# First product of the convolution and the square of the GELU moved to ScalarE in the recurrent tiles of a decoder step

## The chip, the cores and the metric

The kernel runs on 1 core of one Trainium2 chip. The metric is the device time of one execution in microseconds (us); lower is better. All arithmetic is fp32; matrix products are made of three products of split operands (high by high, high by low, low by high).

## The reference

One inference step of one decoder layer, for a prompt of 1024 tokens and 64 sample tokens (8 sequences of 8) with the same weights: half-step FFN, RMS norm, one input projection `z = h @ w_in`, then three branches (dilated window attention, a recurrent branch, attention into a memory), a gated merge, an output projection, a second half-step FFN and a final norm. The change lies in the recurrent branch, of width 768:

```python
xc, conv_new = causal_conv(xr, conv_buf, conv_w, conv_b)       # width 4, per channel: sum_k w[k]*x[t+k-3] + b
r = sigmoid(xc @ w_a + b_a); i = sigmoid(xc @ w_i + b_i)       # 12 blocks of 64
log_a = -8 * r * softplus(-lam); a = exp(log_a)
u = sqrt(-expm1(2*log_a)) * (i * xc)
h_t = a_t * h_{t-1} + u_t                                      # scan over the positions
y_rec = gelu(yr) * h                                           # 0.5*y*(1+tanh(c*(y + 0.044715*y^3)))
```

## The kernel before

Tokens lie on the free axis (1088 columns, `NT`), features on the 128 partitions. The 1088 columns are worked in three chunks, `CH`, of 352, 368 and 368 columns. `z_tile` (L652) makes one block of 128 output features of the input projection: for each chunk, 24 matmuls (`mac3`, 8 blocks of k by three products) into one PSUM bank, then the evacuation function of the caller, then a `tick`. A tick (L71) also falls inside each `mac3`, so there are two ticks per chunk. At a tick the jobs that `later(n, f)` has put n ticks ahead are written out, and so are the next steps of side jobs: the merging of the attention groups (`att_combine`, L826), and the attention of the sample rows into their caches (`sample_job`, L917), which takes place on all engines in the same stage.

The order of instructions on PE, ScalarE (ACT), VectorE (DVE) and GpSimd (POOL) is the order in which the program writes them (`manual_schedule`, L1568): an engine that waits for an operand holds up all that stands behind it in its own queue.

The weights are loaded raw (`wr`), and `part` (L162) splits each into a high part on ScalarE (L167) and a low part on VectorE (L168); a ring of 7 split tiles (`ws`) stands ahead of PE.

The recurrent stage has 6 tiles of 128 features (`lru_tile`, L1297), each followed by one or two gate tiles (`gate_evac`, L1389), which are ordinary `z_tile`s. One recurrent tile is two `z_tile`s. The first has `conv` as its evacuation: L1312 scales the PSUM bank into `xe`, L1318 makes the first product of the convolution with its bias, and L1321 adds the other three products. Five ticks after, `gates(c)` issues two matmuls on the convolved chunk (L1332, three PSUM banks named `g`) and two sigmoids (L1333). The second `z_tile` has `gelu`: L1367 scales the bank into `Y`, and three POOL instructions (L1369 to L1371) make `y + 0.044715*y^3` in `G`.

After `gates(2)`, at the end of the GELU's second chunk, six jobs follow one tick apart: `tanh` (in the middle of the GELU's last chunk), then `power` (written just behind that chunk's evacuation: L1343, L1345), `root` (L1348), `grow` (L1351), `forcing` and `scan` (L1360). The tanh of the GELU (L1373) and the last products (L1374, L1378) come six to eight ticks after the last chunk, and the tile's result goes to DRAM.

PSUM in this stage: three banks for `z`, two named `t` for transposes and the sample rows, three `g`.

Of the kernel before, what the change touches and what calls it, by code (L numbers as in the profile page):

```python
# [11 lines left out]
AF = mybir.ActivationFunctionType  # L12
OP = mybir.AluOpType
# [21 lines left out]
GELU_C = math.sqrt(2.0 / math.pi)  # L35
# [25 lines left out]
class Kernel:  # L61
# [1235 lines left out]
    def lru_tile(self, i):  # L1297

        nc, p, w = self.nc, self.lp, self.lws[i % 2]
        T = lambda tag, n=LP: p.tile([128, n], F32, name=self.uid(tag), tag=tag, bufs=1)  # L1300
        xe, xc, A, B, S, Y, G = (T(x, n) for x, n in (("xe", LP + 3), ("xc", LP), ("lA", LP), ("lB", LP + 3), ("lS", LP),
                                                      ("lY", NT), ("lG", NT)))
        fin = p.tile([128, 36], F32, name=self.uid("fin"), tag="fin", bufs=1)
        smp = lambda ap: ap[:, SEQ + 3:SEQ + 91].rearrange("p (b u) -> p b u", u=11)
        samp = lambda ap: ap.rearrange("p (b t) -> p b t", b=8)
        nc.gpsimd.memset(xe[:, 0:3], 0.0)
        nc.gpsimd.tensor_copy(smp(xe)[:, :, 0:3], samp(self.stT[:, i, 0:24]))

        def conv(c, ps):
            t0, n = CH[c]  # L1310
            m = min(n, SEQ - t0)
            nc.vector.tensor_tensor(out=xe[:, 3 + t0:3 + t0 + m], in0=ps[:, :m], in1=self.rbc[:, t0:t0 + m], op=OP.mult)  # L1312
            if m < n:
                nc.vector.tensor_tensor(out=smp(xe)[:, :, 3:], in0=samp(ps[:, m:n]), in1=samp(self.rbc[:, SEQ:]),
                                        op=OP.mult)
            a, W = LCH[c]
            xo = xc[:, a:a + W]
            nc.vector.tensor_scalar(xo, xe[:, a:a + W], self.col("conv_w", i), self.col("conv_b", i),  # L1318
                                    op0=OP.mult, op1=OP.add)
            for k in range(1, 4):  # L1320
                nc.vector.scalar_tensor_tensor(xo, xe[:, a + k:a + k + W], self.col("conv_w", k * KR + i), xo,  # L1321
                                               op0=OP.mult, op1=OP.add)
            if m < n:
                nc.gpsimd.tensor_copy(fin[:, 0:3], xe[:, SEQ:SEQ + 3])
                nc.gpsimd.tensor_copy(fin[:, 3:27].rearrange("p (b w) -> p b w", b=8), smp(xe)[:, :, 8:11])
            self.later(5, lambda: gates(c))

        def gates(c):
            a, W = LCH[c]
            for j, (dst, name) in enumerate(((A, "lru_b_a"), (B, "lru_b_i"))):  # L1330
                pg = self.bank("g")
                nc.tensor.matmul(pg[:, :W], w[:, j, :], xc[:, a:a + W], start=True, stop=True)  # L1332
                nc.scalar.activation(dst[:, a:a + W], pg[:, :W], AF.Sigmoid, bias=self.col(name, i))  # L1333
            if c == 2:
                for n, f in enumerate((tanh, power, root, grow, forcing, scan)):
                    self.later(1 + n, f)

        def tanh():
            nc.scalar.activation(S, A, AF.Tanh, scale=self.c4[:, i:i + 1])
            nc.vector.tensor_tensor(out=xc, in0=xc, in1=B[:, :LP], op=OP.mult)  # L1340

        def power():
            nc.scalar.activation(A, A, AF.Exp, scale=self.cq[:, i:i + 1])  # L1343
            for _ in range(2):
                nc.scalar.activation(A, A, AF.Square)  # L1345

        def root():
            nc.scalar.activation(S, S, AF.Sqrt)  # L1348

        def grow():  # L1350
            nc.vector.scalar_tensor_tensor(S, A, 1.0, S, op0=OP.add, op1=OP.mult)  # L1351

        def forcing():
            nc.vector.tensor_tensor(out=S, in0=S, in1=xc, op=OP.mult)
            starts = slice(SEQ + 2, SEQ + 80, 11)
            nc.vector.memset(A[:, starts], 0.0)
            nc.vector.tensor_copy(S[:, starts], self.stT[:, i, 24:32])

        def scan():
            nc.vector.tensor_tensor_scan(B[:, :LP], A, S, 0.0, op0=OP.mult, op1=OP.add)  # L1360
            nc.gpsimd.tensor_copy(fin[:, 27:28], B[:, SEQ - 1:SEQ])
            nc.gpsimd.tensor_copy(fin[:, 28:36], B[:, SEQ + 10:SEQ + 88:11])
            nc.sync.dma_start(self.o["fin"][i], fin)

        def gelu(c, ps):
            t0, n = CH[c]
            nc.vector.tensor_tensor(out=Y[:, t0:t0 + n], in0=ps[:, :n], in1=self.rbc[:, t0:t0 + n], op=OP.mult)  # L1367
            y, g = Y[:, t0:t0 + n], G[:, t0:t0 + n]
            nc.gpsimd.tensor_tensor(out=g, in0=y, in1=y, op=OP.mult)  # L1369
            nc.gpsimd.tensor_scalar(g, g, 0.044715, 1.0, op0=OP.mult, op1=OP.add)  # L1370
            nc.gpsimd.tensor_tensor(out=g, in0=g, in1=y, op=OP.mult)  # L1371
            if c == 2:
                self.later(6, lambda: nc.scalar.activation(G, G, AF.Tanh, scale=GELU_C))  # L1373
                self.later(7, lambda: nc.vector.scalar_tensor_tensor(Y, G, 1.0, Y, op0=OP.add, op1=OP.mult))  # L1374
                self.later(8, gated)

        def gated():
            nc.vector.scalar_tensor_tensor(Y[:, :SEQ], Y[:, :SEQ], 0.5, B[:, :SEQ], op0=OP.mult, op1=OP.mult)  # L1378
            nc.vector.scalar_tensor_tensor(samp(Y[:, SEQ:]), samp(Y[:, SEQ:]), 0.5, smp(B)[:, :, 0:8],
                                           op0=OP.mult, op1=OP.mult)  # L1380
            nc.sync.dma_start(self.y_d[6 + i], Y)

        self.z_tile(conv)
        if i + 1 < KR:
            self.lru_weights(i + 1)
        self.z_tile(gelu)


# [570 lines left out]
```

## Time and profile before

| what | us |
|---|---|
| median of the three runs | 2753.1 |
| lowest of the three runs | 2748.8 |
| the profiled execution, its own time | 2744.7 |
| span of the profiled execution (first to last instruction) | 2742.9 |
| mean granted TensorE clock of the profiled execution, of full speed | 0.99 |

The profiled execution is one more run, taken with the profiler; its own time is 1.8 us above its span. The rows below come from it. PE is the matmul engine and PEld its weight loads, which overlap; DVE is VectorE, ACT is ScalarE, POOL is GpSimd, SP the queue of most DMAs. "Idle before" is the time in which an engine stood still ahead of an instruction, with the instruction that ended it.

### The profile page before, as it was taken

The numbers are of one execution on the slowest core, as the hardware profiler recorded it, in microseconds if no ns is written. First come the engines' busy times: TensorE is split into PE (matmuls) and PEld (weight loads), VectorE is DVE, ScalarE is ACT, GpSimd is POOL, SyncE is SP. The second block draws the span as 40 slices with busy tenths as digits, with TensorE's granted clock in tenths as the row PEclk, the third lists the DMA queues.
The fourth block names the chain that finished last, engine by engine and source line by source line (L and its number), as shares of the span: only waits on it lengthen the run. The fifth ranks groups of instructions, "written<-read, shape, count | busy, mean of one in ns | idle before, by whom it ended". The sixth has DMA issues, their size and how long they took to land.

```text
span 2742.9 us, 46310 instructions
## 1 busy us (share of the span) xinstructions
PE 2657.4 (97%) x18088; PEld 2576.8 (94%) x18088; DVE 1718.3 (63%) x3032; ACT 923.3 (34%) x1779; POOL 818.2 (30%) x743
## 2 busy tenths in 40 slices
PE   8999999899999999999989999999999999999997
PEld 7999999899999899989978889999999999999997
DVE  7666566777774433556587755863666566576776
ACT  7232323311153312333334533522542232242112
POOL 1365545200030000324353411231025555552003
PEclk9999999999999999999999999999999999999998
DMA  4222323522243252655544443754424455445221
GB/s 150 70 94 84 103 101 108 205 95 93 75 163 129 89 156 75 204 184 161 177 154 135 138 135 97 264 176 161 149 99 174 163 186 189 168 158 173 95 73 66
DMA packets 181404, 374.98 MB, mean 137 GB/s; under 512 B 21768, under 2 KB 116168, under 8 KB 180416
## 3 DMA queue, kind: packets, MB, share of 16 engines
q1 hardware_dynamic: 166464, 303.85, 33.6%
q0 software_dynamic: 2048, 43.65, 4.7%
q10 hardware_dynamic: 12672, 24.52, 2.4%
q8 instruction: 142, 2.33, 0.4%
q14 instruction: 78, 0.64, 0.1%
HBM read 305.59 MB, written 113.16 MB: 153 GB/s over the span
## 4 chain that ended last, share of the span: by engine, by line
PE 82%; DVE 9%; ACT 3%; issue 2%; DMA 2%; POOL 1%; SPq 0%; DVEq 0%; ACTq 0%; POOLq 0%
PE pg L262 9%; PE pg L264 9%; PE pg L263 9%; PE z L262 7%; PE z L263 7%; PE z L264 7%; PE pd L262 6%; PE pd L263 6%; PE pd L264 6%; DVE ws L168 2%; PE po L264 2%; PE po L263 2%; PE po L262 2%; PE wo L262 1%; PE wo L263 1%
## 5 line engine op out<-in xcount | busy, mean ns | idle before, releaser
L262 PE MATMUL pg<-xo,ws 128*128 128x272 f32 x2512 | 729.4, 290 | 19.8 <-DVE uu L539 10.9
L264 PE MATMUL pg<-xo,ws 128*128 128x272 f32 x2512 | 726.1, 289 | 6.1 <-DVE ws L168 6.1
L263 PE MATMUL pg<-xo,ws 128*128 128x272 f32 x2512 | 725.8, 289 | 0.0
L167 ACT ACTIVATE ws<-wr 128x512 fp32r<-128x512 f32 (+1 forms) x550 | 325.4, 613 | 844.7 <-PE pd L264 363.7
L168 DVE TENSOR_TENSOR ws<-wr,ws 128x512 fp32r<-128x512 f32 (+1 forms) x550 | 436.6, 816 | 137.4 <-ACT ws L167 136.8
L262 PEld LDWEIGHTS pg<-xo,ws 128*128 128x128 f32 x2512 | 475.6, 189 | 23.0 <-DVE uu L539 13.0
L264 PEld LDWEIGHTS pg<-xo,ws 128*128 128x128 f32 x2512 | 475.7, 189 | 7.0 <-DVE ws L168 6.9
L262 PE MATMUL z<-xg,ws 128*128 128x368 f32 (+1 forms) x1392 | 477.4, 343 | 0.0
L263 PEld LDWEIGHTS pg<-xo,ws 128*128 128x128 f32 x2512 | 475.9, 189 | 0.0
L264 PE MATMUL z<-xg,ws 128*128 128x368 f32 (+1 forms) x1392 | 459.0, 330 | 0.0
L263 PE MATMUL z<-xg,ws 128*128 128x368 f32 (+1 forms) x1392 | 458.8, 330 | 0.0
L262 PE MATMUL pd<-h,ws 128*128 128x368 f32 (+1 forms) x1056 | 347.3, 329 | 5.6 <-DVE x L648 4.5
L263 PE MATMUL pd<-h,ws 128*128 128x368 f32 (+1 forms) x1056 | 346.1, 328 | 0.0
L264 PE MATMUL pd<-h,ws 128*128 128x368 f32 (+1 forms) x1056 | 345.0, 327 | 0.0
L648 DVE TENSOR_TENSOR x<-x,pd 128x368 f32<-128x368 f32 (+1 forms) x504 | 257.7, 529 | 137.7 <-PE pd L264 136.0
L262 PEld LDWEIGHTS z<-xg,ws 128*128 128x128 f32 x1392 | 264.1, 190 | 15.6 <-issue 13.9
L263 PEld LDWEIGHTS z<-xg,ws 128*128 128x128 f32 x1392 | 264.3, 190 | 1.3
L264 PEld LDWEIGHTS z<-xg,ws 128*128 128x128 f32 x1392 | 263.4, 189 | 0.0
L262 PEld LDWEIGHTS pd<-h,ws 128*128 128x128 f32 x1056 | 198.1, 188 | 6.5 <-DVE x L648 5.1
L264 PEld LDWEIGHTS pd<-h,ws 128*128 128x128 f32 x1056 | 198.7, 188 | 0.0
L263 PEld LDWEIGHTS pd<-h,ws 128*128 128x128 f32 x1056 | 198.4, 188 | 0.0
L978 POOL TENSOR_TENSOR qb<-qb,kv 128x1024 f32<-128x1024 f32 x48 | 116.3, 2424 | 194.2 <-DMA qb<-qs_d 152.3
(295 smaller groups left out, 3692.3 us busy)
## 6 DMA issues: line engine op xcount, KB each, us to landing
wr<-in_w_gu_dram SPq DMA_DIRECT2D x96, 512.0 KB
wr<-in_w_in_dram SPq DMA_DIRECT2D x58, 512.0 KB
qb<-qs_d SPq DMA_DIRECT2D x48, 512.0 KB
h_d<-sl ACTq DMA_DIRECT2D x88, 272.0 KB
hr<-h_d SPq DMA_DIRECT2D x44, 544.0 KB
wr<-in_w_dn_dram SPq DMA_DIRECT2D x44, 512.0 KB
out_sk_dram<-in_cache_k_dram POOLq DMA_DIRECT2D x16, 1020.0 KB, 7.0
out_sv_dram<-in_cache_v_dram POOLq DMA_DIRECT2D x16, 1020.0 KB, 8.2
```

The costliest lines, as they stand in the source:

```text
L167: nc.scalar.activation(spl[:, 0, :n], src, AF.Copy)
L168: nc.vector.tensor_tensor(out=spl[:, 1, :n], in0=src, in1=spl[:, 0, :n].bitcast(F32), op=OP.subtract)
L262: nc.tensor.matmul(out, wh, xh, start=start and i == 0, stop=False, **more)
L263: nc.tensor.matmul(out, wh, xl, start=False, stop=False, **more)
L264: nc.tensor.matmul(out, wl, xh, start=False, stop=i == n - 1, **more)
L648: nc.vector.tensor_tensor(out=xa, in0=xa, in1=ps[:, :n], op=OP.add)
L978: nc.gpsimd.tensor_tensor(out=prev, in0=prev, in1=kk, op=OP.mult)
```

## The change

In `conv`, the first product with its bias goes from a VectorE `tensor_scalar` to one ScalarE activation (Identity, with scale and bias read per partition). In `gelu`, the POOL instructions are dropped: the square is a ScalarE activation, and one VectorE instruction makes `(y^2 + 1/0.044715) * y`; the factor 0.044715 goes into the scale of the tanh that follows. Nothing else moves: each new instruction is written at the place of the old one.

```diff
-            nc.vector.tensor_scalar(xo, xe[:, a:a + W], self.col("conv_w", i), self.col("conv_b", i),
-                                    op0=OP.mult, op1=OP.add)
+            nc.scalar.activation(xo, xe[:, a:a + W], AF.Identity, bias=self.col("conv_b", i), scale=self.col("conv_w", i))
             for k in range(1, 4):
                 nc.vector.scalar_tensor_tensor(xo, xe[:, a + k:a + k + W], self.col("conv_w", k * KR + i), xo,
                                                op0=OP.mult, op1=OP.add)
...
             y, g = Y[:, t0:t0 + n], G[:, t0:t0 + n]
-            nc.gpsimd.tensor_tensor(out=g, in0=y, in1=y, op=OP.mult)
-            nc.gpsimd.tensor_scalar(g, g, 0.044715, 1.0, op0=OP.mult, op1=OP.add)
-            nc.gpsimd.tensor_tensor(out=g, in0=g, in1=y, op=OP.mult)
+            nc.scalar.activation(g, y, AF.Square)
+            nc.vector.scalar_tensor_tensor(g, g, 1 / 0.044715, y, op0=OP.add, op1=OP.mult)
             if c == 2:
-                self.later(6, lambda: nc.scalar.activation(G, G, AF.Tanh, scale=GELU_C))
+                self.later(6, lambda: nc.scalar.activation(G, G, AF.Tanh, scale=GELU_C * 0.044715))
```

## Rows read from the trace of the kernel before

**Rows 1.** The page's first part: busy time, share of the span and number of instructions of each engine over the whole run.

```profile
PE 2657.4 (97%) x18088; PEld 2576.8 (94%) x18088; DVE 1718.3 (63%) x3032; ACT 923.3 (34%) x1779; POOL 818.2 (30%) x743
```

**Rows 2.** Busy time of each engine in stretches of the recurrent stage (1380 to 1700 us; the view of windows). Columns: stretch and its length, busy us (instructions) of PE, PEld, DVE, ACT and POOL, granted TensorE clock, busy share of the DMA engines, GB/s.

```profile
1380.00:1700.00 320.00, 300.25 (x1858) 269.63 (x1857) 218.34 (x432) 142.72 (x207) 110.76 (x152) 0.98 0.40 124
...
1380.00:1430.00 50.00, 38.98 (x224) 36.62 (x222) 43.98 (x63) 20.35 (x25) 32.51 (x25) 0.96 0.45 143
1580.00:1630.00 50.00, 50.00 (x324) 43.74 (x323) 25.31 (x48) 21.61 (x31) 8.67 (x12) 1.00 0.44 138
1430.00:1435.00 5.00, 2.95 (x11) 2.91 (x12) 2.99 (x6) 3.53 (x8) 2.13 (x8) 0.50 0.08 23
1490.00:1495.00 5.00, 5.00 (x22) 5.00 (x22) 2.06 (x11) 2.01 (x5) 3.22 (x5) 0.66 0.44 112
```

**Rows 3.** What the matmul engine PE waited for between 1375 and 1700 us (the view of waits): who waited and for whom, total us, times, longest us.

```profile
PE t L1020 <- ACT ss L1012: 8.9, 1, 8.9
PE g L1332 <- DVE xc L1321: 4.2, 2, 2.7
PE t L835 <- DVE ss L1009: 3.5, 1, 3.5
PE t L835 <- DVE sel L1047: 2.9, 2, 2.0
```

**Rows 4.** The instructions that the change removes or feeds, each asked by its line: number, shortest/median/longest duration in ns, first and last start in us, shapes.

```profile
L1318 DVE TENSOR_SCALAR xc<-xe,vec x18: 462/471/2380, 1384.8 to 1661.3; 128x352 f32<-128x352 f32 x6, 128x368 f32<-128x368 f32 x6, 128x392 f32<-128x392 f32 x6
L1321 DVE SCALAR_TENSOR_TENSOR xc<-xe,vec,xc x54: 583/602/2627, 1387.3 to 1663.2; 128x352 f32<-128x352 f32 x18, 128x368 f32<-128x368 f32 x18, 128x392 f32<-128x392 f32 x18
L1369 POOL TENSOR_TENSOR lG<-lY x18: 773/800/912, 1403.9 to 1677.1; 128x368 f32<-128x368 f32 x12, 128x352 f32<-128x352 f32 x6
L1370 POOL TENSOR_SCALAR lG<-lG x18: 487/500/821, 1404.8 to 1678.0; 128x368 f32<-128x368 f32 x12, 128x352 f32<-128x352 f32 x6
L1371 POOL TENSOR_TENSOR lG<-lG,lY x18: 940/985/2007, 1405.4 to 1678.6; 128x368 f32<-128x368 f32 x12, 128x352 f32<-128x352 f32 x6
```

**Rows 5.** ScalarE operations of the nearest shapes (the view of groups by line, shapes kept apart): count, busy us, mean ns, then idle us before them and its releasers. L1453 has no per-partition pointer operand, L281 has one (its scale), L319 is a square, the last row is one table load.

```profile
L1453 ACT ACTIVATE xg<-ta 128x368 fp32r<-128x368 f32 x16 | 8.2, 513 | 24.7 <-POOL ta L1465 24.7
L281 ACT ACTIVATE xg<-x,vec 128x368 fp32r<-128x368 f32 x16 | 9.6, 600 | 5.5 <-DVE x L648 4.8 <-DVE rs L290 0.8
L319 ACT ACTIVATE td<-x 128x368 f32<-128x368 f32 x25 | 12.6, 504 | 7.4 <-POOL acc L321 4.0 <-DVE x L648 2.3 <-DVE rs L290 1.1
L1348 ACT ACT_TABLE_LOAD x6 | 7.7, 1283 | 0.1
```

**Rows 6.** Single instructions of POOL and VectorE (DVE) in the first recurrent tile (the view by time): start us, length us, engine and line, operation, tiles and shapes, count, and in brackets the idle time before it with its releaser.

```profile
1384.63 2.38 POOL L978 TENSOR_TENSOR qb<-qb,kv 128x1024 f32<-128x1024 f32 x1 [0.27 <-DMA qb<-qs_d]
1384.84 2.38 DVE L1318 TENSOR_SCALAR xc<-xe,vec 128x352 f32<-128x352 f32 x1
1414.57 1.22 DVE L968 TENSOR_REDUCE sst<-qb 128x16 f32<-128x1024 f32 x1 [2.80 <-POOL qb L978]
1418.64 2.60 DVE L1351 SCALAR_TENSOR_TENSOR lS<-lA,lS 128x1112 f32<-128x1112 f32 x1 [0.41 <-ACT lS L1348]
```

**Rows 7.** The same view in the second recurrent tile, ScalarE (ACT), VectorE and PE: the table load with which the chain of exponentials begins, the evacuation of the GELU's last chunk, a later evacuation, and the wait of PE at the tile's end.

```profile
1457.46 1.28 ACT L1343 ACT_TABLE_LOAD   x1
1460.55 0.54 DVE L1367 TENSOR_TENSOR lY<-z,rbc 128x368 f32<-128x368 f32 x1 [1.87 <-PE z L264]
1469.99 0.54 DVE L1393 TENSOR_TENSOR ta<-z,rbc 128x368 f32<-128x368 f32 x1 [1.08 <-PE z L264]
1489.00 0.21 DVE L1009 TENSOR_TENSOR ss<-t,sbn 128x64 f32<-128x64 f32 x1
1489.23 0.41 PE L835 MATMUL t<-ident,oc 128*128 128x128 f32 x2 [3.49 <-DVE ss L1009]
```

**Rows 8.** The same view in the other tiles (first, third, fourth, fifth, sixth): the first ScalarE instruction of the chain of exponentials (L1343) and the evacuation of the GELU's last chunk (L1367).

```profile
1410.27 1.28 ACT L1343 ACT_TABLE_LOAD   x1
1411.24 0.53 DVE L1367 TENSOR_TENSOR lY<-z,rbc 128x368 f32<-128x368 f32 x1
1513.13 1.23 ACT L1343 ACTIVATE lA<-lA,spw 128x1112 f32<-128x1112 f32 x1
1561.84 1.23 ACT L1343 ACTIVATE lA<-lA,spw 128x1112 f32<-128x1112 f32 x1
1562.27 0.54 DVE L1367 TENSOR_TENSOR lY<-z,rbc 128x368 f32<-128x368 f32 x1
1616.66 1.28 ACT L1343 ACT_TABLE_LOAD   x1
1619.27 0.54 DVE L1367 TENSOR_TENSOR lY<-z,rbc 128x368 f32<-128x368 f32 x1 [2.86 <-PE z L264]
1674.20 1.28 ACT L1343 ACT_TABLE_LOAD   x1
1676.51 0.54 DVE L1367 TENSOR_TENSOR lY<-z,rbc 128x368 f32<-128x368 f32 x1 [2.09 <-PE z L264]
```

**Rows 9.** The same view, in the fifth tile the instruction that frees a PSUM bank and the matmuls that take that bank next, and in the sixth tile the transposes at the end of the sample rows' attention.

```profile
1631.56 0.40 DVE L1047 TENSOR_TENSOR sel<-t,sel 128x256 f32<-128x256 f32 x1
1634.00 0.56 PE L1006 MATMUL t<-sk,sqz 128*128 128x64 f32 x4
1697.82 0.66 PE L1068 MATMUL t<-ident,ogl 128*64 128x128 f32 x8
```

## The prediction

> **What bounds the kernel now.** I read the page first: PE is busy for 97% of the span, no other engine for more than 63% [rows 1]. So time can be lost or won only where PE stands still or runs at a lower clock. Then I cut out the stage of the six recurrent tiles with the view of windows, because only there does the change add or remove an instruction. Of its 320 us PE is busy 300.25; VectorE is busy 218.3 and ScalarE 142.7, so they have 101.7 and 177.3 us free [rows 2]. The stage has two halves: in the first 50 us PE works 38.98 and VectorE 43.98, later PE works all 50.00 of a 50 us stretch [rows 2]. The waits of PE name what it lacked: once 8.9 us for an exponential on ScalarE that itself follows VectorE, and 4.2 + 3.5 + 2.9 us for VectorE, together 19.5 us [rows 3]. After the longest wait the granted clock is 0.50 for five microseconds (the 1.2 GHz level), and after the 3.49 us wait its mean is 0.66 [rows 2, 7]. Against full speed that costs 0.50 x 2.95 + 0.34 x 5 = 3.2 us. Nothing in this stage can therefore give back more than 19.5 + 3.2 = 22.7 us, which is 0.8% of the run.
>
> **What goes.** Eighteen VectorE products of 0.471 us median, 8.5 us, and from POOL 18 x (0.800 + 0.500 + 0.985) = 41.1 us [rows 4]. None of it ran on PE. POOL's work there was hidden by PE's matmuls, except in the first tile, where VectorE waited 2.80 us for a POOL product (L978) that stood behind GELU instructions [rows 6].
>
> **What comes.** The trace before has no Identity. The nearest rows are a copy without a pointer operand, 0.513 us, and one with a pointer scale, 0.600 [rows 5]: 0.087 for one pointer, so 0.687 with two. The bounds are 0.513 (pointers cost nothing) and 0.774 (each costs double); I take 0.687, the straight continuation. The square is 0.504 [rows 5], and the VectorE step is like L1321, 0.602 [rows 4]; it lies between 0.583 and 2.63, the longest L1321, which met a POOL instruction. A handoff from one engine to another is about 0.02: L1009 ends at 1489.21, PE starts at 1489.23 [rows 7]. On ScalarE this is 18 x (0.687 + 0.504) = 21.4 us, far below its 177 free.
>
> One rule speaks against the move. The products go from a 0.471 us VectorE row to an estimated 0.687 on ScalarE. The Trainium skill (ScalarE: Activation LUTs, Rules for kernel authors) advises VectorE for multiplies and adds; these rows agree with it, and by them the moved product itself loses 18 x 0.216 = 3.9 us of engine time.
>
> **The new waits.** Queues run in the order written, so each of the 36 places now has VectorE standing still until ScalarE is done.
> In `conv` VectorE is held for 0.02 + 0.687 + 0.02 where it worked 0.471: 0.26 more a chunk, 4.7 in all. In `gelu` it is held and then works, 0.02 + 0.504 + 0.02 + 0.602 = 1.15 a chunk, 20.7 in all; behind it wait the weights' low parts (L168), the other evacuations and the sample rows. Both lie within VectorE's 101.7 free microseconds; if that cover were gone they would cost 25.4 us.
>
> The costlier wait is on ScalarE. The chain of exponentials (`power`, `root`) is written behind the GELU's last chunk. Before, ScalarE had nothing to do in that chunk and began the chain early. Now a square that waits for L1367 stands ahead of it, and of all that hangs on the chain: L167, `root`, `grow`, the scan, and through them the evacuations and the sample rows' PSUM banks. The delay is the end of L1367 + 0.52 - the old start of the chain. By tile:
> - First: L1367 ended at 1411.77 [rows 8]. Two earlier chunks hold VectorE for 2.3; I let half of it be repaid by a shorter wait for POOL [rows 6], 1.2 left. 1411.77 + 1.2 + 0.52 - 1410.27 = 3.2 us, and it lands on the 8.9 us wait [rows 3].
> - Second: 1461.09 + 0.52 - 1457.46 = 4.15; VectorE was idle 1.08 later, and two `conv` chunks add 0.52: 3.6 us more on the 3.49 us wait [rows 7].
> - Third: ScalarE came late anyway (1513.13 [rows 8]); only the square and one `conv` chunk, 0.5 + 0.26 = 0.8, which lands on the last of the 2.9 us.
> - Fourth: 1562.81 + 0.52 - 1561.84 = 1.5 [rows 8], without a wait of PE near it: 0.
> - Fifth: 1619.81 + 0.52 - 1616.66 = 3.7. The bank freed at 1631.96 is free at 1635.6, and PE wants it at 1634.0 [rows 8, 9]: 1.6.
> - Sixth: 1677.05 + 0.52 - 1674.20 = 3.4; PE's transposes at 1697.82 close this chain [rows 8, 9]. I take 2.0, between nothing and 3.4.
>
> The delays add up to 16.4 us on ScalarE, and 3.2 + 3.6 + 0.8 + 0 + 1.6 + 2.0 = 11.2 us of it reach PE. The profiled execution's own 2744.7 becomes 2755.9. The median of the runs shown is 2753.1, 8.4 above that execution, the lowest 2748.8; by the median the same sum would be 2764. The range covers both. No DMA is added, removed or moved; the tile's store follows its chain.
>
> **The rivals.**
> *Hidden anyway:* PE runs ahead by up to three `z` banks and seven split weights, and every delay ends under its matmuls. For it: PE busy 300.25 of 320, VectorE a third free. Against it: the waits of rows 3 are exactly at the ends of these chains. It gives the old 2744.7, give or take 4.
>
> *POOL's relief wins:* a VectorE product of 0.471 took 2.38 when a POOL product had begun 0.21 earlier [rows 4, 6]; the Identity isn't in that contest, and L978 comes sooner; `grow` (L1351), held to 2.60 in the first tile, may be shorter too [rows 6]. Half of the 22.7 us back gives 2733, all of it 2722. Against it: the instructions that collide here are L978's, which stay, and three L1321 still meet them. The Trainium skill (SBUF — State Buffer, section on the two separate sides) says that VectorE and GpSimd take a shared port pair as an exclusive lock for a whole instruction, and that ScalarE never waits for it; the 2.38 us row agrees, and by that rule alone this rival would be the likely one.
>
> *VectorE becomes the bound:* no cover at all, 25.4 + 16.4 = 41.8 more, 2786.5. Against it: the 101.7 free.
>
> *Slower by over 2%, table loads:* if Identity needed a table of its own, every `conv` chunk would bring a load and one back, 36 x 1.283 = 46.2 [rows 5] on the way to the convolved chunk, and with 11.2 that is 2802.1. It decides from 34 loads on (54.9 - 11.2 = 43.7 us). Against it, squares and scaled copies stand among exponentials and tanhs here without a load of their own. The Trainium skill (ScalarE: Activation LUTs, Table sets) says that identity is in every set; no run so far shows it.
>
> **How the numbers follow.** Forecast (some of the chain's delay reaches PE, 2747 to 2770) 0.45; hidden 0.25; relief 0.20; VectorE the bound 0.07; table loads 0.03. The likeliest gives 2756. The range, 2736 to 2783, takes in the forecast, the hidden case, the nearer half of the relief and of VectorE as bound; it leaves out some 0.18. A measurement of this kernel can tell about 2% from no change, 54.9 us. More than that can't be won in this stage (22.7 at most): 0.01 for what I have not seen. Slower by over 2% is the table loads, 0.03. Within 2%: 0.96.
>
> **What would show it.** In the profile after: Identity at about 0.69 and the square at 0.50, without new table loads (right), or loads on their lines (wrong). The first L1343 of the second tile some 4 us later against L1367 than before, right behind the square; if it still comes ahead of the evacuation, the mechanism is wrong. The waits of PE: 8.9 to about 12, 3.5 to about 7; if they shrink, the relief has won. POOL's busy time about 41 less, with the span not following. PE's busy time for the same matmuls should not change; if the stage outside 1380 to 1700 us changes by more than a few microseconds, the prediction is wrong in a way that none of these cases covers.

## The result and the profile after

| | kernel before | changed kernel |
|---|---|---|
| median, us | 2751.35 (5 runs) | 2765.79 (5 runs, 2764.72 to 2766.03) |
| ratio, 95% interval | 1 | 1.0056 [1.0045, 1.0067] |
| span of the profiled execution, us | 2742.9 | 2763.1 |

The change costs 0.56%, 15.4 us of 2751.35. By 2% that is the same; by the interval it is a small loss, clear of the noise. One of the five runs of the kernel before took 4307.2 us; the median counts it and the ratio leaves it out, so the medians alone differ by 14.4 us and not by 15.4. The page of the changed kernel, busy time by engine, answers to [rows 1]:

```profile
PE 2666.6 (97%) x18088; PEld 2585.0 (94%) x18088; DVE 1710.8 (62%) x3032; ACT 941.1 (34%) x1815; POOL 774.4 (28%) x689
```

POOL lost 43.8 us of work and the run grew. Where it grew is read by cutting both traces at the same two events: the start of the last exponential of the window attention (L792), ahead of the recurrent tiles, and the merge's first evacuation into `tb` (L1461), behind them. These are the views of windows, first of the kernel before, then of the changed kernel; the columns are those of [rows 2].

```profile
0.00:1342.90 1342.90, 1305.52 (x8976) 1259.78 (x8977) 809.28 (x1447) 435.62 (x948) 353.52 (x299) 0.99 0.38 124
1342.90:1733.70 390.80, 370.57 (x2286) 339.64 (x2286) 248.68 (x474) 164.52 (x248) 127.97 (x159) 0.98 0.46 144
1733.70:2742.90 1009.20, 981.31 (x6830) 977.36 (x6828) 660.31 (x1113) 323.20 (x586) 336.72 (x285) 0.99 0.44 151
```

```profile
0.00:1346.30 1346.30, 1307.42 (x8975) 1261.37 (x8976) 808.41 (x1447) 435.38 (x948) 352.73 (x299) 0.99 0.38 124
1346.30:1749.40 403.10, 373.68 (x2286) 342.05 (x2286) 241.30 (x474) 182.52 (x284) 84.37 (x105) 0.97 0.45 140
1749.40:2763.10 1013.70, 985.51 (x6830) 981.57 (x6828) 661.12 (x1113) 323.18 (x586) 337.27 (x285) 0.99 0.44 150
```

The stage takes 403.1 us instead of 390.8, 12.3 more. The parts around it hold the same instructions and yet differ by 3.4 and 4.5 us; that is how far one execution stands from another, since over all ten profiled executions of this study the first part takes 1342.0 to 1347.5 and the last 1009.2 to 1013.7. In the stage PE was idle for 20.2 us before and 29.4 after (length less busy), 9.2 more; the other 3.1 us are the same 2286 matmuls at a lower mean clock, 0.97 instead of 0.98 (the last section shows where).

The waits of PE in the changed kernel, 1375 to 1720 us, answer to [rows 3]:

```profile
PE t L1020 <- ACT ss L1012: 8.2, 1, 8.2
PE t L835 <- DVE ss L1009: 4.8, 2, 3.7
PE t L835 <- DVE sel L1047: 3.6, 2, 2.3
PE t L1068 <- POOL ogl L876: 3.5, 1, 3.5
PE g L1331 <- DVE xc L1320: 2.7, 1, 2.7
PE g L1331 <- ACT lA L1332: 2.6, 1, 2.6
PE t L1006 <- DVE sel L1047: 2.8, 2, 1.9
PE t L835 <- issue: 0.8, 1, 0.8
```

No wait became much longer; new ones came. The transposes at the end of the sample rows (L1068) now wait 3.5, the banks that L1047 frees are late twice (L1006), and the gate matmuls wait 2.6 for a sigmoid.

The new instructions, each asked by its line (lines behind 1318 stand one lower than before, behind 1369 two):

```profile
L1318 ACT ACTIVATE xc<-xe,vec x18: 679/696/716, 1388.3 to 1673.9; 128x352 f32<-128x352 f32 x6, 128x368 f32<-128x368 f32 x6, 128x392 f32<-128x392 f32 x6
L1368 ACT ACTIVATE lG<-lY x18: 492/510/513, 1406.0 to 1689.4; 128x368 f32<-128x368 f32 x12, 128x352 f32<-128x352 f32 x6
L1369 DVE SCALAR_TENSOR_TENSOR lG<-lG,lY x18: 524/543/945, 1406.5 to 1689.9; 128x368 f32<-128x368 f32 x12, 128x352 f32<-128x352 f32 x6
L1332 ACT ACT_TABLE_LOAD  x8: 1283/1283/1283, 1399.2 to 1674.6; - x8
```

They are as long as expected, within 0.01 us on ScalarE and 0.06 less on VectorE, and the new lines carry no table load. The cost is in the order. Here is the second tile by time, the place of [rows 7]: ScalarE, then VectorE and PE.

```profile
1466.88 0.51 ACT L1368 ACTIVATE lG<-lY 128x368 f32<-128x368 f32 x1 [3.54 <-DVE lY L1366]
1467.40 1.28 ACT L1342 ACT_TABLE_LOAD   x1
```

```profile
1466.30 0.54 DVE L1366 TENSOR_TENSOR lY<-z,rbc 128x368 f32<-128x368 f32 x1 [2.48 <-PE z L264]
...
1472.81 1.29 DVE L168 TENSOR_TENSOR ws<-wr,ws 128x512 fp32r<-128x512 f32 x2 [4.51 <-ACT ws L167]
```

```profile
1477.57 0.41 PE L835 MATMUL t<-ident,oc 128*128 128x128 f32 x2 [1.29 <-DVE sel L1047]
...
1494.05 0.66 PE L1006 MATMUL t<-sk,sqz 128*128 128x64 f32 x4 [1.92 <-DVE sel L1047]
1498.38 0.66 PE L835 MATMUL t<-ident,oc 128*128 128x128 f32 x2 [3.67 <-DVE ss L1009]
```

The square makes ScalarE wait 3.54 us for the evacuation L1366, which waits for PE. Right behind it the table load opens the chain of exponentials. In [rows 7] that load began 3.09 us ahead of the evacuation (1457.46 against 1460.55), now 1.10 behind it. VectorE then stands 4.51 us for a weight's high part (L167), which lies behind the chain, and PE pays 1.29 + 1.92 + 3.67 = 6.9 us of waits where it paid 3.49.

### The profile page after: what moved, and what is told of

The parts are those of the page before. It is cut to its first block, busy times and chain, and to the rows that moved or that the text cites. A ratio compares the mean times of both kernels' runs of the same rounds, so it can differ in the third digit from the quotient of the medians.

```text
span 2763.1 us, 46280 instructions
## 1 busy us (share of the span) xinstructions
PE 2666.6 (97%) x18088; PEld 2585.0 (94%) x18088; DVE 1710.8 (62%) x3032; ACT 941.1 (34%) x1815; POOL 774.4 (28%) x689
## 4 chain that ended last, share of the span: by engine, by line
PE 81%; DVE 9%; ACT 4%; issue 2%; DMA 2%; POOL 1%; SPq 0%; DVEq 0%; ACTq 0%; POOLq 0%
PE pg L262 9%; PE pg L264 9%; PE pg L263 9%; PE z L262 7%; PE z L263 6%; PE z L264 6%; PE pd L262 6%; PE pd L263 6%; PE pd L264 6%; DVE ws L168 2%; PE po L264 2%; PE po L263 2%; PE po L262 2%; PE wo L262 1%; PE wo L263 1%
## 5 line engine op out<-in xcount | busy, mean ns | idle before, releaser
L262 PE MATMUL pg<-xo,ws 128*128 128x272 f32 x2512 | 730.8, 291 | 21.3 <-DVE uu L539 11.2
L167 ACT ACTIVATE ws<-wr 128x512 fp32r<-128x512 f32 (+1 forms) x550 | 325.3, 613 | 846.2 <-PE pd L264 366.1
L262 PEld LDWEIGHTS z<-xg,ws 128*128 128x128 f32 x1392 | 264.8, 190 | 15.7 <-issue 14.0
L978 POOL TENSOR_TENSOR qb<-qb,kv 128x1024 f32<-128x1024 f32 x48 | 115.0, 2398 | 205.1 <-DMA qb<-qs_d 145.0
```

The costliest lines, as they stand in the source:

```text
L167: nc.scalar.activation(spl[:, 0, :n], src, AF.Copy)
L262: nc.tensor.matmul(out, wh, xh, start=start and i == 0, stop=False, **more)
L978: nc.gpsimd.tensor_tensor(out=prev, in0=prev, in1=kk, op=OP.mult)
```

## The experiments

The theory: the ScalarE square of the GELU's last chunk pushes the chain of exponentials behind that chunk's evacuation, and this is nearly the whole loss. The first rival: each of the 36 handoffs between VectorE and ScalarE costs alike. The second: what POOL gave up is worth something, and hides part of the loss or could be won.

Two numbers stand beside each ratio: the length of the stage, cut as above, and the start of the first exponential of the chain (`power`) less the start of the last chunk's evacuation, for the six tiles in order.

| kernel | ratio [95%] | stage, us | chain less evacuation, us |
|---|---|---|---|
| before | 1 | 390.8 | 0.32, -1.79, 1.58, -0.43, -1.31, -1.02 |
| changed | 1.0056 [1.0045, 1.0067] | 403.1 | 2.38, 2.40, 1.71, 0.99, 2.40, 2.40 |
| convolution alone | 1.0005 [0.9996, 1.0014] | 392.3 | 0.97, -1.79, 1.58, -0.43, -1.32, -1.01 |
| GELU alone | 1.0052 [1.0040, 1.0065] | 405.1 | 2.39, 2.40, 1.72, 0.99, 2.40, 2.40 |
| chain first | 1.0005 [0.9996, 1.0013] | 393.1 | 0.29, -1.58, 1.45, -2.11, -1.32, -0.88 |
| GELU deferred | 1.0002 [0.9993, 1.0011] | 392.2 | -0.11, -1.39, 0.32, -0.77, -1.12, -0.62 |
| square alone | 1.0050 [1.0036, 1.0063] | 403.7 | 2.39, 2.40, 1.85, 0.98, 2.40, 2.39 |
| deferred GELU alone | 1.0010 [1.0001, 1.0018] | 395.0 | -2.22, -1.39, 0.32, -0.77, -1.12, -0.61 |
| deferred, zeros on VectorE | 1.0004 [0.9996, 1.0013] | 392.5 | -0.62, -1.40, 0.32, -0.77, -1.12, -0.61 |
| POOL's GELU left out | 0.9988 [0.9978, 0.9997] | 389.4 | -2.06, -1.78, 0.32, -1.17, -1.32, -1.01 |

Ratios are to runs of the kernel before on the same chip, whose medians were 2748.5 to 2751.4.

**Convolution alone.** Against the kernel before:

```diff
-            nc.vector.tensor_scalar(xo, xe[:, a:a + W], self.col("conv_w", i), self.col("conv_b", i),
-                                    op0=OP.mult, op1=OP.add)
+            nc.scalar.activation(xo, xe[:, a:a + W], AF.Identity, bias=self.col("conv_b", i), scale=self.col("conv_w", i))
```

> Only the first product of the convolution goes to ScalarE; the GELU stays on POOL as before. Theory (the chain of exponentials is pushed behind the last square, that is the main cost): no square, so only the 18 holds of VectorE of 0.26 us and what they do at the banks: 1 to 4 us above the kernel before. Rival (each of the 36 handoffs costs alike): half of them are here, so half of the 15.5 us, 7 to 8. Second rival (the chip spreads such small differences anyway): no difference outside the run-to-run spread.

Measured: 1.4 us above (-1.1 to 3.8). Eighteen of the handoffs cost 3.8 at most, half of what the rival needs.

**GELU alone.** Against the changed kernel, the first product goes back to VectorE (the diff above, reversed).

> Only the GELU changes (square on ScalarE, one step on VectorE); the first product stays on VectorE. Theory: the pushed chain is all here, 9 to 13 us above the kernel before. Rival (handoffs alike): 7 to 8. The two parts should add up to about 15.5 if they do not interact.

Measured: 14.3 us above (11.0 to 17.9), one microsecond more than the theory's window and nearly twice the rival's 7 to 8. The two parts add to 15.7, the whole is 15.4.

**Chain first.** Against the changed kernel, `power` is written in the tick of `tanh`:

```diff
-                for n, f in enumerate((tanh, power, root, grow, forcing, scan)):
-                    self.later(1 + n, f)
+                for n, f in ((1, tanh), (1, power), (3, root), (4, grow), (5, forcing), (6, scan)):
+                    self.later(n, f)
```

> The whole change, but the exponential and its two squares (power) are written one tick earlier, ahead of the evacuation of the GELU's last chunk and so ahead of its square on ScalarE. Theory: the old start of the chain comes back, and with it most of the cost of the second, fifth and sixth tile (3.6, 1.0 and 3.4 us) and some of the first: 2 to 7 us above the kernel before, instead of 15.5. Rival (handoffs): all 36 are still there, so 15 as with the change.

Measured: 1.4 us above (-1.1 to 3.6), less than the theory's 2. All 36 handoffs are still in it; in the second tile the VectorE step even waits longer for its square than in the changed kernel, 1.87 against 0.58, here in its view by time:

```profile
1464.06 0.54 DVE L1369 SCALAR_TENSOR_TENSOR lG<-lG,lY 128x368 f32<-128x368 f32 x1 [1.87 <-ACT lG L1368]
```

So a hold of VectorE is cheap and the chain is dear; the first rival falls. The waits of PE show which ones left:

```profile
PE t L1020 <- ACT ss L1012: 6.1, 1, 6.1
...
PE g L1331 <- ACT lA L1332: 2.6, 1, 2.6
PE t L1068 <- POOL ogl L876: 0.7, 1, 0.7
PE t L1006 <- DVE sel L1047: 0.2, 1, 0.2
```

L1068 waits 0.7 instead of 3.5, L1006 0.2 instead of 2.8. The 2.6 us for the sigmoid stay, and cost nothing in sum: L1020 waits 6.1 instead of 8.2.

**GELU deferred.** Against the changed kernel:

```diff
-            nc.scalar.activation(g, y, AF.Square)
-            nc.vector.scalar_tensor_tensor(g, g, 1 / 0.044715, y, op0=OP.add, op1=OP.mult)
+            self.later(1, lambda: nc.scalar.activation(g, y, AF.Square))
+            self.later(2, lambda: nc.vector.scalar_tensor_tensor(g, g, 1 / 0.044715, y, op0=OP.add, op1=OP.mult))
```

> The whole change, but the square is written one tick and its VectorE step two ticks after the evacuation, so that the square stands behind the chain of exponentials and VectorE is held by no square. Theory: as with the chain first or a little better, 0 to 5 us above the kernel before. Rival (handoffs alike): the 18 of the GELU are gone, the 18 of the convolution stay, 7 to 8.

Measured: 0.5 us above (-1.9 to 3.0), at the theory's low end.

**Square alone.** Against the kernel before, one line; the square is made again by POOL, so it does nothing but stand there:

```diff
             y, g = Y[:, t0:t0 + n], G[:, t0:t0 + n]
+            if c == 2:
+                nc.scalar.activation(g, y, AF.Square)
             nc.gpsimd.tensor_tensor(out=g, in0=y, in1=y, op=OP.mult)
```

> The kernel before, with one square of the GELU's last chunk on ScalarE added in each tile at the place where the change has it (6 squares of 0.5 us; POOL then makes the same square again, so the result does not depend on them). Nothing else is changed: no Identity, no new VectorE step, POOL keeps its work. Theory (the chain of exponentials stands behind a square that waits for the evacuation): 7 to 12 us above the kernel before, with the chain of the second tile starting about 4 us later against L1367. Rival (the loss comes from VectorE's holds and from what POOL no longer does): 0 to 2 us.

Measured: 13.7 us above (9.9 to 17.3). The theory's window was 7 to 12: the cause is the one it named, its size was put too low. Six instructions of 0.51 us, none of which computes anything new, bring nine tenths of the loss. Its second tile, ScalarE by time, is that of the changed kernel:

```profile
1464.89 0.51 ACT L1370 ACTIVATE lG<-lY 128x368 f32<-128x368 f32 x1 [3.67 <-DVE lY L1367]
1465.42 1.28 ACT L1343 ACT_TABLE_LOAD   x1
```

So are the waits of PE:

```profile
PE t L1068 <- POOL ogl L876: 3.5, 1, 3.5
...
PE t L1006 <- DVE sel L1047: 2.5, 2, 1.7
```

**Deferred GELU alone.** Against the kernel with the GELU deferred, the first product goes back to VectorE.

> Only the GELU's part, with its square one tick and its VectorE step two ticks after the evacuation; the first product stays on VectorE. In the trace of the run with the deferred GELU one wait of PE was left that comes from an Identity ahead of the sigmoids (2.6 us, for a gate bank). Theory: that wait goes too, and with POOL's 41 us of work gone from the stage the time is 0 to 6 us below the kernel before. Rival (the wait is caught by the next one, 5.5 us for the sample rows' exponential): the same as the kernel before, within 2 us.

Measured: 2.7 us above (0.3 to 4.9). The theory's gain didn't come; by the interval it is even slightly slower than the kernel before. The 2.6 us wait for the gate bank is gone, but L1020 waits 7.8 us, where it waited 5.5 in the kernel with the Identity:

```profile
PE t L1020 <- ACT ss L1012: 7.8, 1, 7.8
PE t L835 <- DVE ss L1009: 3.5, 1, 3.5
PE g L1332 <- DVE xc L1321: 3.3, 1, 3.3
```

**Deferred, zeros on VectorE.** Against the kernel with the GELU deferred:

```diff
-        nc.gpsimd.memset(xe[:, 0:3], 0.0)
+        nc.vector.memset(xe[:, 0:3], 0.0)
```

> The whole change with the deferred GELU, and the three zeros ahead of the first convolved column written by VectorE instead of POOL, because the first Identity of the profiled run waited until 1388.29 us for POOL's memset, 1.9 us after its own evacuation. Theory: the first convolved chunk is ready up to 1.7 us earlier, but PE's 5.5 us wait later in that tile takes it back: within 2 us of the kernel with the deferred GELU, 0 to 3 us above the kernel before. Rival (that wait sets the end): 1.7 us less than it.

Measured: 1.1 us above (-1.1 to 3.6), as with POOL's zeros. It says little: in the profiled execution with POOL's zeros and the GELU deferred, the first Identity waited for its evacuation, not for the zeros.

**POOL's GELU left out.** Against the kernel before; the cubic term of the GELU is missing from its result:

```diff
-            nc.gpsimd.tensor_tensor(out=g, in0=y, in1=y, op=OP.mult)
-            nc.gpsimd.tensor_scalar(g, g, 0.044715, 1.0, op0=OP.mult, op1=OP.add)
-            nc.gpsimd.tensor_tensor(out=g, in0=g, in1=y, op=OP.mult)
...
-                self.later(6, lambda: nc.scalar.activation(G, G, AF.Tanh, scale=GELU_C))
+                self.later(6, lambda: nc.scalar.activation(G, Y, AF.Tanh, scale=GELU_C))
```

> The kernel before with the three POOL instructions of the GELU left out and nothing put in their place: the tanh reads y itself, so the cubic term of the GELU is missing from the result. It measures POOL's relief alone, 41 us of POOL work without any new wait. Rival of the prediction (POOL's relief wins): 5 to 20 us below the kernel before. Theory (POOL's work lay beside PE's, the waits of PE are set by VectorE and ScalarE): 0 to 4 us below.

Measured: 3.3 us below (0.8 to 6.0). That is what the 41 us of POOL work can give when nothing comes in their place. Its stage by windows and the waits that stay:

```profile
1380.00:1700.00 320.00, 303.88 (x1867) 273.26 (x1866) 214.34 (x432) 142.69 (x207) 66.85 (x98) 0.97 0.39 125
```

```profile
PE t L1020 <- ACT ss L1012: 7.3, 1, 7.3
PE t L835 <- DVE ss L1009: 3.5, 1, 3.5
PE g L1332 <- DVE xc L1321: 3.5, 1, 3.5
PE t L835 <- DVE sel L1047: 1.6, 1, 1.6
```

Of 19.5 us of waits in [rows 3], 15.9 are still there without POOL's GELU. No version that computes the reference was faster than the kernel before.

## Why the prediction was right

**The mechanism was the one named.** The square alone brings 13.7 of 15.4 us, and writing the chain ahead of it takes 14 of them away. The chain's delay against the evacuation, from the table above, sums to 14.9 us over the six tiles; the prediction had 16.4. Its own six delays, with 3.6 for the second tile, add up to 16.2. Two more slips in it change nothing: the 8.5 us of VectorE products is 18 times their median, while they took 12.6 in sum; and 34 table loads come to 43.6 us, so they would decide from 35 on.

**The size, tile by tile.** The reading takes one matmul of PE near the end of each tile in both traces; what its start has moved beyond the mark of the tile before is put down to that tile. The stage begins 3.4 late.

| tile | PE's mark | before | after | moved | of it in this tile | predicted |
|---|---|---|---|---|---|---|
| first | L1020 | 1432.05 | 1437.45 | 5.40 | 2.0 | 3.2 |
| second | L835 | 1489.23 | 1498.38 | 9.15 | 3.8 | 3.6 |
| third | L835 | 1538.79 | 1548.88 | 10.09 | 0.9 | 0.8 |
| fourth | L835 | 1570.01 | 1581.18 | 11.17 | 1.1 | 0 |
| fifth | L1006 | 1634.00 | 1646.21 | 12.21 | 1.0 | 1.6 |
| sixth | L1068 | 1697.82 | 1713.51 | 15.69 | 3.5 | 2.0 |

The sum is 12.3 against 11.2, but with misses of both signs in it.
- First tile: the chain's start moved by 1416.92 - 1410.27 - 3.4 = 3.25 us, as predicted (3.2). What it forgot is in its own rows: `grow` had taken 2.60 us beside a POOL product [rows 6]; starting later it took 1.32, which returns 1.28. The prediction let this count for the rival only. The forecast of 8.9 growing to 12 failed for another reason as well: PE came to that wait later, by 2.7 us beyond the 3.4. Its waits for the gate banks took 1.1 us more (2.66 + 2.58 against 2.68 + 1.49), and behind the second of them it worked at a lower granted clock (0.66 from 1400 to 1405), which took the rest.
- That bank was not in the prediction. The Identity of the third chunk and the square of the first stand ahead of sigmoids that free PSUM banks of the gates, the same kind of wait as with the chain. It cost nothing in sum here, because L1020 shortened.
- Second tile: the sum was right, the place was not. The wait of 3.49 was to grow to about 7 and stayed at 3.67; the delay came as two new waits for banks that L1047 frees (1.29 and 1.92), the rest by the clock.
- Third tile: 0.9 against 0.8 is luck. The wait that was to grow went from 2.04 to 2.28 only. What moved the mark is the clock behind the second tile's wait: these are the 5.60 us from the second tile's mark on, before and after. At 0.70 and at 0.54 PE loses 1.7 and 2.6 us of them and does 25 and 20 matmuls.

```profile
1489.23:1494.83 5.60, 5.60 (x25) 5.60 (x26) 2.74 (x15) 2.31 (x5) 3.22 (x5) 0.70 0.39 100
```

```profile
1498.38:1503.98 5.60, 5.60 (x20) 5.60 (x21) 2.74 (x15) 1.03 (x4) 3.21 (x5) 0.54 0.36 100
```

- Fourth tile: "without a wait of PE near it" was wrong. L835 waits 1.18 us for VectorE (L1009) where it had no wait before.
- Sixth tile: the 2.0 was chosen between 0 and 3.4; all of it arrived (3.5).

**The prices held.** Identity 0.696 (0.687 predicted), square 0.510 (0.504), hold of VectorE in `gelu` 11.2 / 18 = 0.62 idle and 0.543 work, 1.16 (1.15). As predicted, this is covered: VectorE is busy 241 of 403 us.

**Where the total came out higher.** 2765.8 against 2755.9 is 9.9 us. Of these, 6.7 are the base: the sum was made on an execution of 2744.7, and the median is 2751.35. The rest is the change itself, 14.4 between the medians (15.4 by the ratio) against 11.2. In the stage 12.3 can be placed; what is left lies within what two single executions differ by outside the stage, and no run here locates it. The prediction also held PE's busy time for fixed. In the stage it grew by 3.1 us, through the clock (below), and it is part of the 12.3.

**The rivals.** *Hidden anyway* fails by the interval. *POOL's relief* is real and small, 3.3 us without any new wait. The row of `grow` that spoke for it says less than it seemed to. It took 2.60 with POOL's product L978 beside it and 1.32 in the changed kernel; but it took 1.32 with the square alone too, where POOL keeps its GELU, and 1.97 without POOL's GELU, where L978 still ran beside its first 0.8 us. In these runs its length follows where L978 falls, not whether POOL's GELU is there. That the waits of PE end on VectorE did not make them POOL's: 15.9 of 19.5 us stay. These are `grow` in the first tile of the changed kernel, with the square alone, and without POOL's GELU:

```profile
1425.30 1.32 DVE L1350 SCALAR_TENSOR_TENSOR lS<-lA,lS 128x1112 f32<-128x1112 f32 x1 [1.24 <-ACT lS L1347]
```

```profile
1423.16 1.32 DVE L1351 SCALAR_TENSOR_TENSOR lS<-lA,lS 128x1112 f32<-128x1112 f32 x1 [0.78 <-ACT lS L1348]
```

```profile
1417.62 1.97 DVE L1351 SCALAR_TENSOR_TENSOR lS<-lA,lS 128x1112 f32<-128x1112 f32 x1 [1.24 <-ACT lS L1348]
```

*VectorE the bound* would have shown in the chain-first kernel, which keeps every hold and loses 1.4 us. *Table loads* did not come: 8 on the sigmoids' line before and after, 28 in the whole stage in both, and none on the Identity's line. The Trainium skill (ScalarE: Activation LUTs, Table sets) has it that identity is in every set; the trace agrees.

## What to carry to other kernels

Before moving an operation to an engine with free time, read what stands behind it in that engine's queue. An instruction that must wait for a late operand turns the free time in front of it into a delay of all that follows: six squares of 0.5 us cost 13.7 (9.9 to 17.3). With the GELU's squares written one tick later the whole change costs 0.5 (-1.9 to 3.0), and the GELU's part by itself 2.7 (0.3 to 4.9). Judge such a move by the order, tile by tile against the marks of the bounding engine, and not by the engine's busy share.

## What the runs showed of the hardware

The VectorE step with a constant took 0.543 us at 368 columns in the changed kernel (the median of L1369), while L1321 with a per-partition scalar took 0.602 there in the kernel before (its mean at that shape); the prediction had taken 0.602 for both.

At three of PE's standstills the granted clock fell to the lower level, and PE's wait is then not the whole price. At another, the 3.52 us of L1068, it did not (1.00 from 1710 to 1720). By windows of five microseconds in the changed kernel, around the waits of 2.58, 8.2 and 3.67 us:

```profile
1400.00:1405.00 5.00, 3.93 (x12) 3.38 (x13) 4.93 (x6) 2.48 (x5) 3.27 (x4) 0.66 0.65 195
...
1430.00:1435.00 5.00, 0.00 (x0) 0.00 (x0) 4.99 (x8) 0.81 (x2) 4.84 (x4) 0.69 0.10 38
1435.00:1440.00 5.00, 2.55 (x9) 2.52 (x10) 2.90 (x7) 3.08 (x6) 2.52 (x8) 0.50 0.03 4
1440.00:1445.00 5.00, 5.00 (x25) 5.00 (x25) 4.12 (x8) 0.84 (x2) 0.00 (x0) 0.79 0.70 253
...
1495.00:1500.00 5.00, 1.62 (x6) 1.65 (x7) 4.49 (x18) 0.99 (x4) 0.00 (x0) 0.67 0.01 3
1500.00:1505.00 5.00, 5.00 (x21) 5.00 (x21) 1.31 (x6) 0.21 (x1) 3.21 (x5) 0.64 0.40 112
```

0.50 is the 1.2 GHz level; the mean of 0.64 in a window in which PE is busy throughout means that it worked part of it at that level, 21 matmuls instead of the 30 of the next five microseconds (1505 to 1510). Working time lost that way: 0.34 x 3.93 + 0.50 x 2.55 + 0.21 x 5 + 0.33 x 1.62 + 0.36 x 5 = 6.0 us. Before, it is 3.7: the 3.2 read from [rows 2], and 0.10 x 5 in the window right behind the first of theirs:

```profile
1435.00:1440.00 5.00, 5.00 (x29) 5.00 (x29) 4.79 (x10) 1.00 (x1) 0.00 (x0) 0.90 0.63 236
```

These 2.3 us are most of the 3.1 by which PE's busy time grew in the stage. The stretch at 1400 to 1405, which the kernel before lacks in its profiled execution, does not need the change: without POOL's GELU, in a kernel faster than before, the clock stood at 0.66 from 1390 to 1395.
